# Attention values projected with tokens on partitions, page units that count as landed only with a slack, and probabilities that stay in one place

## The chip, the cores and the metric

One core of a Trainium2 chip runs the whole program. The metric is the device time of one execution in microseconds (us); for the kernel before, three runs gave 854.75, 854.88 and 855.74 us, a median of 854.88 us. The profile shown below is of one more execution of that kernel.

The core has these engines, each with its own instruction stream that runs in order: PE (matrix multiply, with a weight load stream PEld beside it), DVE (vector), ACT (scalar), POOL (general), and SP, which here only issues DMA transfers. They wait for each other through semaphores.

## The reference, cut to what matters

One inference step of a decoder layer: 256 prompt tokens and 64 sample tokens (8 requests of 8 tokens) go through one input projection of 2048 into 8272 columns; three groups of heads work on its parts; their outputs, each times a gate, go through one output projection and a layer norm. What the change touches is the value part of the first group, `av`:

```python
z = jnp.einsum('btd,dn->btn', h, w)            # tokens x 2048 by 2048 x 8272
aq, ak, av, ag, iq, ik, iw, bq, bf, bi, bg, mq, mg = jnp.split(z, cuts, axis=-1)
av = av.reshape(n_b, n_t, H_A, DH_A)           # 8 heads of 128 columns
...
p = jax.nn.softmax(s, axis=-1)
return jnp.einsum('bthk,btkhd->bthd', p, v_sel.astype(jnp.float32))
```

The prompt attends with a mask of its selected keys over its own 256 tokens. The sample tokens attend over 2048 cached keys and values each, read from pages in device memory, and over their own new keys and values. `av` itself is an output too, for prompt and sample tokens.

## The kernel before

All 320 tokens stand side by side: `xh` and `xl` hold the transposed input as a high and a low part, 16 blocks of 128 model dimensions, 320 tokens each. Every weight tile (`wr`, 512 KB, by DMA from SP) is also split, into `wh` (ACT copies, which rounds) and `wl` (DVE or POOL subtracts). A product is the sum of three PE passes: wh with xh, wh with xl, wl with xh.

Most of the input projection is done by units of 128 output columns ("T" in `pe_quantum`): the weight block is the stationary operand, the 320 tokens are streamed, and a PSUM tile `pj` (two buffers) collects 16 x 3 matmuls of 128x320. The result has columns on partitions and tokens along the row. The eight heads of `av` are eight such units; `ev_av` copies each to a tile `AV[h]` and stores it to the output `vT`. `attn_values` then turns each head by three PE transposes into tokens on partitions (`avn`; the new sample values go to `avS`), and multiplies it with the transposed probabilities.

The output projection works the other way round: the tokens are the stationary operand (three groups: tokens 0 to 127, 128 to 255, and the 64 sample tokens whose high and low part stand side by side), and 512 weight columns are streamed.

Between the quanta of the projection the PE does page units (`unit`): K units score the queries against pages of cached keys, V units multiply probabilities with pages of cached values. Each unit takes four page DMAs of 512 KB, into tiles `pg` (five buffers) or `S`. Their matmuls use 32 stationary columns at a time. A unit in one piece with the next is a pair.

No hardware queue decides the order. While the program is built, a planner (`Plan`) keeps an estimated clock for every engine; the main loop emits at each estimated moment whatever its rules call ready: background work (`bg`: the indexer, attention scores, softmax, recurrence), then page units (`units_now`), then the next projection quantum (`half_ready`), else it moves its clock on. The planner's clock is no wait on the chip. There the order is fixed and each instruction waits for its real inputs alone, so that an error of an estimate shows up as a wait of an engine behind the late instruction. `loads` sets the order of the DMAs on SP in the same way.

In the same stretch of the program DVE runs `topk_sample`: 32 rounds of a MAX8 and a MATCH_REPLACE8 over 1032 columns.

Of the kernel before, what the change touches and what calls it, by code (L numbers as in the profile page):

```python
# [47 lines left out]
IDLE = 3.0  # L48
LOOK = 3
# [96 lines left out]
class Engine:  # L146
# [41 lines left out]
    def cost(self, op, outs, ins, n):  # L188
        if self.name == "PE":
# [8 lines left out]
            if a.dtype == F32R:  # L198
                return turn + 0.0087 + n * 0.0004325
# [11 lines left out]
        f = 1.0  # L211
# [17 lines left out]
def hymba_step(ctx: ExitStack, tc: tile.TileContext, I, O):  # L229
# [199 lines left out]
    def ev_av(h):  # L429
        def f(ps):  # L430
            AV[h] = T()
            ACT.copy(AV[h], ps)
            store(O["vT"][h], AV[h])
            done.add(("av", h))
        return f
# [17 lines left out]
    def pad_queries():  # L453
        yield from wait(("mq", 0))
# [70 lines left out]
    def add_block(kind, i):  # L525
# [3 lines left out]
        elif kind == "mem":  # L529
            for k in range(16):  # L530
                wspec.append(dict(kind="mem", k=k, n=1024, nq=2, src=I["wm"][:, k, :]))
        else:
            base, ev = {"iq": (32, ev_iq), "aq": (0, ev_aq), "ak": (8, ev_ak), "av": (16, ev_av), "mq": (56, ev_mq),
# [128 lines left out]
    def page_tag(n):  # L662
# [3 lines left out]
        if (len(PG) - len(in_s) + ("q" in st) + ("more" in st) + ci_live(0) < BUFS["pg"]  # L666
                and plan.slot_free("pg", BUFS["pg"]) <= plan.now + 0.2):
            return "pg"
# [53 lines left out]
    def unit(n):  # L722
# [21 lines left out]
        elif kind == "V":  # L744
            if u == 0:
                VACC[p] = PS([128, 512], "va")
            for j in range(2):
# [31 lines left out]
    def unit_ready(n):  # L779
        kind, p, u = punits[n]  # L780
        if any((n, b) not in PG or plan.avail(PG[n, b]) > plan.now for b in range(2)):
# [5 lines left out]
        if kind == "V":  # L787
            return ("soft", p) in done and plan.avail(PTt[p]) <= plan.now and (u < 7 or "attn" in done) and (
# [8 lines left out]
    def loaded(n):  # L797
        return all((n, b) in PG and plan.avail(PG[n, b]) <= plan.now for b in range(2))
# [350 lines left out]
    def attn_scores():  # L1149
        yield from wait("pbias", "idxdone")  # L1150
        for h in range(8):
            yield from wait(("aq", h), ("ak", h))
            yield from room(2)
# [4 lines left out]
            P0, P1, s8 = T(128), T(256), T8()  # L1158
# [1113 lines left out]
```

## Time and profile before

| | us |
|---|---|
| median of three runs | 854.88 |
| the profiled execution, its own time | 854.57 |
| its span, first to last instruction | 852.8 |
| PE busy | 843.1 (99%) |
| DVE busy | 553.9 (65%) |
| ACT busy | 422.3 (50%) |
| POOL busy | 326.0 (38%) |
| DMA: hardware queue's share of 16 engines | 83.6% |

A PE row of the profile ends later than the next one starts, since matmuls are pipelined: the `pj` rows show a mean of 306 to 316 ns on the page, though they start closer together. So the cost of a matmul here is not its mean duration but the distance from one start to the next, which the chain of waits gives as a piece's time by its count. Matmuls of full fp32 operands have two rows each (three of them are `x6`); those on the split operands, and transposes, have one. PE's granted clock is 1.00 but in the last slice, when it has ended.

### The profile page before, as it was taken

What the parts mean: (1) busy time and instruction counts of PE and PEld (TensorE: products, weight loads), DVE (VectorE), ACT (ScalarE), POOL (GpSimd) and SP (SyncE); (2) the same over time, 40 slices, a digit from 0 to 9 for tenths busy, and PEclk for the clock granted to TensorE, in tenths of its full rate; (3) what the DMA queues carried; (4) which work ended last, traced back from release to release, by engine and by line L of the source; (5) the groups of instructions that cost most, each with busy time, mean ns of one, the idle gap of its engine ahead of it and who ended that gap; (6) DMA issues with size and microseconds to landing.
All of it is one profiled execution on the core that took longest, in us unless ns stands there. A gap on an engine that the chain in (4) does not pass through costs nothing.

```text
span 852.8 us, 19150 instructions
## 1 busy us (share of the span) xinstructions
PE 843.1 (99%) x6892; PEld 718.0 (84%) x6892; DVE 553.9 (65%) x1100; ACT 422.3 (50%) x908; POOL 326.0 (38%) x333
## 2 busy tenths in 40 slices
PE   9999999999999999999999999999999999999996
PEld 8999999877889898878778788787887889888885
DVE  7788897744897898654474556557545343953655
ACT  6454565553555543634544554554444353744432
POOL 0677562564634445331142214333311110714424
PEclk9999999999999999999999999999999999999998
DMA  9567456889999999999989999999999988756633
GB/s 342 172 189 228 156 172 251 279 307 411 376 389 397 335 327 359 398 360 403 389 330 409 408 353 389 401 397 377 347 409 400 364 324 291 272 171 199 195 99 123
DMA packets 83216, 266.49 MB, mean 312 GB/s; under 512 B 10481, under 2 KB 21170, under 8 KB 82482
## 3 DMA queue, kind: packets, MB, share of 16 engines
q1 hardware_dynamic: 82098, 263.18, 83.6%
q0 software_dynamic: 1024, 2.10, 0.8%
q8 instruction: 54, 0.88, 0.4%
q14 instruction: 40, 0.33, 0.1%
HBM read 256.50 MB, written 8.73 MB: 311 GB/s over the span
## 4 chain that ended last, share of the span: by engine, by line
PE 98%; DMA 1%; DVE 0%; SPq 0%; ACT 0%; DVEq 0%; issue 0%
PE pj L157 57%; PE mB L157 13%; PE va L157 10%; PE mA L157 10%; PE kv L157 8%; DMA S<-in_first 1%; DVE pg L157 0%; SPq L157 0%; ACT xh L157 0%; ACT PT L157 0%; DVE s L157 0%; DVEq L2258 0%; DVE avn L157 0%
## 5 line engine op out<-in xcount | busy, mean ns | idle before, releaser
L157 ACT CAST wh<-wr 128x512 fp32r<-128x512 f32 x334 | 205.0, 621 | 243.5 <-PE pj L157 183.9
L157 PE MATMUL pj<-xh,wh 128*128 128x320 f32 (+1 forms) x992 | 313.6, 316 | 0.0
L157 PE MATMUL pj<-xh,wl 128*128 128x320 f32 (+1 forms) x992 | 303.9, 306 | 0.0
L157 PE MATMUL pj<-xl,wh 128*128 128x320 f32 (+1 forms) x992 | 303.8, 306 | 0.0
L157 DVE TENSOR_TENSOR wl<-wr,wh 128x512 fp32r<-128x512 f32 x222 | 172.7, 785 | 181.9 <-ACT wh L157 166.5
L157 POOL TENSOR_TENSOR wl<-wr,wh 128x512 fp32r<-128x512 f32 x112 | 151.0, 1357 | 240.2 <-ACT wh L157 222.7
L157 PEld LDWEIGHTS pj<-xh,wh 128*128 128x128 f32 x992 | 186.7, 188 | 16.0 <-issue 12.5
L157 PEld LDWEIGHTS pj<-xl,wh 128*128 128x128 f32 x992 | 186.8, 188 | 1.3
L157 PEld LDWEIGHTS pj<-xh,wl 128*128 128x128 f32 x992 | 186.6, 188 | 0.0
L157 POOL TENSOR_TENSOR t<-t,t 128x256 f32<-128x256 f32 (+3 forms) x53 | 46.2, 873 | 119.5 <-ACT t L157 60.0
L157 PE MATMUL va<-pg,PT 128*32 128x512 f32 x456 | 58.4, 595 | 0.0
L157 PE MATMUL kv<-pg,qpad 128*32 128x256 f32 (+1 forms) x916 | 57.5, 380 | 0.0
L157 PEld LDWEIGHTS kv<-pg,qpad 128*32 128x32 f32 (+1 forms) x916 | 30.8, 110 | 20.4 <-issue 1.3
L157 PEld LDWEIGHTS va<-pg,PT 128*32 128x32 f32 x456 | 14.6, 109 | 30.4 <-issue 28.1
L157 DVE MAX8 PT<-PT 128x8 f32<-128x1032 f32 x32 | 39.5, 1234 | 0.5
L157 DVE MATCH_REPLACE8 PT<-PT 128x1032 f32<-128x1032 f32 x32 | 39.0, 1218 | 0.0
L157 POOL DMA_INDIRECT S<-in_ci,row x24 | 25.5, 1064 | 20.0 <-DVE row L157 10.6
L157 PE MATMUL mB<-t,wh 128*128 128x256 f32 x128 | 24.5, 289 | 0.0
L157 POOL TENSOR_TENSOR bp<-t,bp 128x128 f32<-128x128 f32 (+1 forms) x17 | 10.7, 627 | 36.0 <-ACT bp L157 36.0
L157 DVE TENSOR_TENSOR cat<-S,cat 64x512 fp32r<-64x512 f32 x24 | 19.5, 813 | 6.9 <-ACT cat L157 6.4
L157 POOL TENSOR_TENSOR t<-t,tabm 128x320 f32<-128x320 f32 x16 | 14.5, 908 | 24.4 <-DVE t L157 24.2
L157 POOL TENSOR_TENSOR xl<-cat,xh 128x256 fp32r<-128x256 f32 x12 | 12.5, 1061 | 24.8 <-ACT xh L157 24.8
(430 smaller groups left out, 1355.0 us busy)
## 6 DMA issues: line engine op xcount, KB each, us to landing
wr<-in_wt SPq DMA_DIRECT2D x124, 512.0 KB
pg<-in_ck SPq DMA_DIRECT2D x114, 512.0 KB
pg<-in_cv SPq DMA_DIRECT2D x114, 512.0 KB
wr<-in_wo SPq DMA_DIRECT2D x36, 512.0 KB
wr<-in_wm SPq DMA_DIRECT2D x16, 512.0 KB
S<-in_ck SPq DMA_DIRECT2D x14, 512.0 KB
S<-in_cv SPq DMA_DIRECT2D x14, 512.0 KB
pg<-in_cXV SPq DMA_DIRECT2D x8, 512.0 KB
```

What stands on the lines that cost most here:

```text
L157: res = f(*a, **k)
```

## The change

The eight `av` units become two chunks of 512 columns, from a weight array `wv` of another layout (the same 16 loads of 512 KB). For each of 16 blocks of model dimensions three accumulators are fed with tokens as the stationary operand: m = 0 and 1, the prompt's two halves, by three matmuls each, and m = 2, the sample tokens, by two (their high and low parts side by side in `xS`, made once by `sample_columns`). m = 0 and 1 use the two `pj` buffers, m = 2 the one `va` buffer that the V units use too. The values come out with tokens on partitions, so that `attn_values` has no transposes and no `avn`; the output is `v`, tokens by columns. V units wait until both chunks' sample values are there.

`attn_scores` writes the probabilities at once to the place in `cat` where their transposes are kept, without tiles from `t`. A page counts as landed for the planner 1.5 us later than before (`PAGE_LAG`), a weight tile's DMA is put on SP only 0.6 us after the planner thinks its buffer free (before: up to 1 us ahead), a constant `cm` is loaded early, in one DMA into a page buffer, and the planner's price of a split matmul is another formula.

```diff
 IDLE = 3.0
+PAGE_LAG = 1.5
 LOOK = 3
...
             if a.dtype == F32R:
-                return turn + 0.0087 + n * 0.0004325
+                return turn + 0.0133 + n / 2400
             if a.dtype == BF:
...
-    def ev_av(h):
-        def f(ps):
-            AV[h] = T()
-            ACT.copy(AV[h], ps)
-            store(O["vT"][h], AV[h])
-            done.add(("av", h))
+    def ev_av(n, m):
+        def f(acc):
+            ps, = acc
+            if m == 2:
+                c = slice(512 * n, 512 * n + 512)
+                ACT.copy(avS[64:128, c], ps[64:128])
+                DVE.tensor_add(avS[64:128, c], avS[64:128, c], ps[0:64])
+                store(O["v"][256:320, c], avS[64:128, c])
+                done.add(("avs", n))
+                return
+            for j in range(2):
+                AV[m, 2 * n + j] = t = T(256)
+                (DVE.tensor_copy if m else ACT.copy)(t, ps[:, 256 * j:256 * j + 256])
+                store(O["v"][128 * m:128 * m + 128, 512 * n + 256 * j:512 * n + 256 * j + 256], t)
+            if m:
+                done.update(("av", h) for h in range(4 * n, 4 * n + 4))
         return f
...
     def pad_queries():
-        yield from wait(("mq", 0))
+        yield from wait(("mq", 0), ("hgrn", 3))
         yield from room(1, "bp")
...
                 wspec.append(dict(kind="mem", k=k, n=1024, nq=2, src=I["wm"][:, k, :]))
+        elif kind == "av":
+            if i % 4 == 0:
+                for k in range(0, 16, 2):
+                    wspec.append(dict(kind="av", nch=i // 4, k=k, n=1024, nq=4,
+                                      src=I["wv"][i // 4, :, k:k + 2, :].rearrange("p a c -> p (a c)")))
         else:
-            base, ev = {"iq": (32, ev_iq), "aq": (0, ev_aq), "ak": (8, ev_ak), "av": (16, ev_av), "mq": (56, ev_mq),
+            base, ev = {"iq": (32, ev_iq), "aq": (0, ev_aq), "ak": (8, ev_ak), "mq": (56, ev_mq),
                         "bf": (44, None), "bq": (40, None), "bi": (48, None), "g": (24, None)}[kind]
...
             return None
-        if (len(PG) - len(in_s) + ("q" in st) + ("more" in st) + ci_live(0) < BUFS["pg"]
+        if (len(PG) - len(in_s) + ("cm" in st) + ("q" in st) + ("more" in st) + ci_live(0) < BUFS["pg"]
                 and plan.slot_free("pg", BUFS["pg"]) <= plan.now + 0.2):
...
                 VACC[p] = PS([128, 512], "va")
+                plan.pinned.add(VACC[p].tensor.name)
             for j in range(2):
...
         kind, p, u = punits[n]
-        if any((n, b) not in PG or plan.avail(PG[n, b]) > plan.now for b in range(2)):
+        if not loaded(n):
             return False
...
         if kind == "V":
-            return ("soft", p) in done and plan.avail(PTt[p]) <= plan.now and (u < 7 or "attn" in done) and (
+            return ("soft", p) in done and ("avs", 1) in done and plan.avail(PTt[p]) <= plan.now and (u < 7 or "attn" in done) and (
                 u or plan.slot_free("va", 1) <= plan.now)
...
     def loaded(n):
-        return all((n, b) in PG and plan.avail(PG[n, b]) <= plan.now for b in range(2))
+        return all((n, b) in PG and plan.avail(PG[n, b]) + PAGE_LAG <= plan.now for b in range(2))
...
             yield from wait(("aq", h), ("ak", h))
-            yield from room(2)
             yield need(AQ[h], AK[h], pbias)
...
             PE.matmul(ps[:, 128:384], AQ[h][:, 128:256], AK[h][:, 0:256], start=True, stop=True)
-            P0, P1, s8 = T(128), T(256), T8()
+            s8, pts = T8(), probs(h)
+            P0, P1 = pts[:, 0:128], pts[:, 128:384]
             DVE.tensor_tensor_reduce(out=P0, in0=ps[:, 0:128], in1=pbias[:, 0:128], scale=-QS, scalar=-FLOOR,
...
             PE.transpose(pt[:, 256:384], P1[:, 128:256], ident)
-            ACT.copy(probs(h), pt)
-            free(P0, P1)
+            ACT.copy(pts, pt)
             done.add(("probs", h))
+    def sample_columns():
+        yield from wait("idxdone")
+        yield from room(2, "bp")
+        xS = [new([128, 8, 128], "bp", F32R) for _ in range(2)]
+        for i in range(2):
+            for x, c in ((xh, 0), (xl, 64)):
+                (DVE.tensor_copy if c else ACT.copy)(xS[i][:, :, c:c + 64], x[:, 8 * i:8 * i + 8, 256:320])
+        st["xS"] = [x.rearrange("p k t -> p (k t)") for x in xS]
...
             yield from wait(("probs", h), ("av", h))
-            yield need(AV[h])
-            avn = new([128, 2, 128], "avn")
-            ps = PS([128, 3, 128])
-            for i in range(2):
-                PE.transpose(ps[:, i, :], AV[h][:, 128 * i:128 * i + 128], ident)
-            PE.transpose(ps[:, 2, :], AV[h][:, 192:320], ident)
-            ACT.copy(avn, ps[:, 0:2, :])
-            ACT.copy(avS[64:128, 128 * h:128 * h + 128], ps[64:128, 2, :])
-            free(AV.pop(h))
-            pts = probs(h)
-            yield need(pts, avn)
+            pts, c = probs(h), slice(128 * (h % 2), 128 * (h % 2) + 128)
+            v0, v1 = (AV[m, h // 2][:, c] for m in range(2))
+            yield need(pts, v0, v1)
             po = PS([128, 256])
-            PE.matmul(po[:, 0:128], avn[:, 0, :], pts[:, 0:128], start=True, stop=True)
-            PE.matmul(po[:, 128:256], avn[:, 0, :], pts[:, 128:256], start=True, stop=False)
-            PE.matmul(po[:, 128:256], avn[:, 1, :], pts[:, 256:384], start=False, stop=True)
+            PE.matmul(po[:, 0:128], v0, pts[:, 0:128], start=True, stop=True)
+            PE.matmul(po[:, 128:256], v0, pts[:, 128:256], start=True, stop=False)
+            PE.matmul(po[:, 128:256], v1, pts[:, 256:384], start=False, stop=True)
             cat_put(h, "p", slice(0, 256), po, ACT.copy)
+            if h % 2:
+                free(*(AV.pop((m, h // 2)) for m in range(2)))
+        yield from wait(("avs", 0), ("avs", 1))
         done.add("attn")
...
                 and plan.slot_free("pj", 2) <= plan.now
+        if s["kind"] == "av":
+            return s["k"] or q or "xS" in st and plan.avail(st["xS"][1]) <= plan.now and not pending and max(plan.slot_free("pj", 2), plan.slot_free("va", 1)) <= plan.now
         if s["kind"] == "mem":
...
                     done.add("lastT")
+        elif s["kind"] == "av":
+            n, K = s["nch"], s["k"] + q // 2
+            ms = ((0, 2), (1,)) if n == K == 0 else ((0,), (1, 2))
+            for m in ms[q % 2]:
+                if K == 0:
+                    pj["av", m] = PS([128, 512], "va" if m == 2 else "pj")
+                ps = pj["av", m]
+                t = slice(128 * m, 128 * m + 128)
+                xS = st["xS"][K // 8][:, 128 * (K % 8):128 * (K % 8) + 128]
+                xs = [(xS, hi), (xS, lo)] if m == 2 else \
+                    [(xh[:, K, t], hi), (xl[:, K, t], hi), (xh[:, K, t], lo)]
+                for x, w in xs:
+                    PE.matmul(ps, x, w, start=K == 0 and x is xs[0][0] and w is hi, stop=K == 15 and w is lo)
+                if n == 1 and K == 15 and m == 2:
+                    free(*st["xS"])
+                if K == 15:
+                    f = ev_av(n, m)
+                    if m == 2:
+                        other_bank.append(f)
+                    pending.append((f, [pj.pop(("av", m))], 0 if m == 2 else 2))
         elif s["kind"] == "mem":
...
     def masks():
-        yield from wait("idxdone")
-        yield from room(2, "bp")
-        cm = [new([128, 1024], "bp"), new([128, 1024], "bp")]
+        yield from wait(("iq", 3))
+        st["cm"] = cm = new([128, 2048], "pg")
         SP.dma_start(lbt[:, 0:8], I["lb"])
         SP.dma_start(ngt, I["ng"])
-        SP.dma_start(cm[0], I["cm"][:, 0:1024])
-        SP.dma_start(cm[1], I["cm"][:, 1024:2048])
-        yield need(*cm, lbt, ngt)
-        ACT.copy(cu8, cm[0][:, 0:304])
-        ACT.copy(emat.rearrange("p a b c d -> p (a b c d)"), cm[1])
-        free(*cm)
+        SP.dma_start(cm, I["cm"])
+        yield need(cm, lbt, ngt, ps=0)
+        yield from idle("ACT", 0.3)
+        ACT.copy(cu8, cm[:, 0:304])
+        ACT.copy(emat.rearrange("p a b c d -> p (a b c d)"), cm[:, 1024:2048])
+        del st["cm"]
         DVE.tensor_scalar(ngt, ngt, -0.5, None, op0=OP.mult)
...
                 continue
-            if nw < len(wspec) and nw < half + 5 and plan.slot_free("wr", 3) <= plan.now + 1 and nw - nprep < 3 \
+            if nw < len(wspec) and nw < half + 5 and plan.slot_free("wr", 3) <= plan.now + (-0.6) and nw - nprep < 3 \
                     and (wspec[nw]["kind"] != "mem" or has_room(3)):
...
     a["first"] = c(first.reshape(128, 8, 1312).transpose(1, 0, 2))
+    a["wv"] = c(w[:, 2048:3072].reshape(16, 128, 2, 512).transpose(2, 1, 0, 3))
     a["wm"] = c(np.concatenate([inp["w_mem_v"][0], inp["w_mem_k"][0]], 1).reshape(16, 128, 1024).transpose(1, 0, 2))
```

The order in which the instructions stand moves with it. First place: PE in the middle of the `av` projection. Before, one head's unit with a piece of attention in it (`ident,t` are the transposes of `AV[h]`, `avn` the values that they made):

```order
L157 MATMUL mA_3295<-ident,t_3217 128x128 x3
L157 MATMUL pj_3207<-xh,wh_3174 128x320
L157 MATMUL pj_3207<-xl,wh_3174 128x320
L157 MATMUL pj_3207<-xh,wl_3175 128x320
L157 MATMUL pj_3207<-xh,wh_3174 128x320
L157 MATMUL pj_3207<-xl,wh_3174 128x320
L157 MATMUL pj_3207<-xh,wl_3175 128x320
L157 MATMUL mB_3315<-cat_468_3148,avn_3294 128x128 x3
```

And now, one block of 128 model dimensions of the second chunk, for all three token groups (`bp` holds `xS`):

```order
L158 MATMUL pj_3669<-wh_3553,xh 128x512
L158 MATMUL pj_3669<-wh_3553,xl 128x512
L158 MATMUL pj_3669<-wl_3554,xh 128x512
L158 MATMUL pj_3681<-wh_3553,xh 128x512
L158 MATMUL pj_3681<-wh_3553,xl 128x512
L158 MATMUL pj_3681<-wl_3554,xh 128x512
L158 MATMUL va_3685<-wh_3553,bp_2934 128x512
L158 MATMUL va_3685<-wl_3554,bp_2934 128x512
```

In all, 384 rows of 128x320 have gone (2688 are 2304) and 256 of 128x512 have come; 24 transposes have gone (184 of 128x128 are 160).

Second place: PE between the two chunks. All three accumulators end within a few rows, and the second chunk needs them free. Between stand one K unit, the products of probabilities and values for heads 0 to 3, and another K unit; these are the rows from the end of the first unit on (`t_3576` and `t_3578` are the tiles that ACT copies from m = 0, `t_3591` and `t_3593` those that DVE copies from m = 1):

```order
L158 MATMUL kv_3597<-pg_3378,qpad_411 32x256 x2
L158 MATMUL mA_3620<-cat_459_3094,t_3576 128x128 x2
L158 MATMUL mA_3620<-cat_459_3094,t_3591 128x128
L158 MATMUL mB_3625<-cat_459_3094,t_3576 128x128 x2
L158 MATMUL mB_3625<-cat_459_3094,t_3591 128x128
L158 MATMUL mB_3630<-cat_459_3094,t_3578 128x128 x2
L158 MATMUL mB_3630<-cat_459_3094,t_3593 128x128
L158 MATMUL mA_3635<-cat_460_3095,t_3578 128x128 x2
L158 MATMUL mA_3635<-cat_460_3095,t_3593 128x128
L158 MATMUL kv_3597<-pg_3489,qpad_411 32x256 x2
```

The two K units around the products were a pair in one piece before; after the second chunk the same stands once more, for heads 4 to 7. Over the whole program, PE enters a stretch of 32-column matmuls 46 times before and 46 times now.

Third place: DVE at the same moment. The two copies of m = 1 and the sum for the sample values stand behind the scores of one head (`ISA`) and a MAX, MATCH_REPLACE round, and before the next round:

```order
L158 MAX PT_487<-PT_487 128x8
L158 MATCH_REPLACE PT_487<-PT_487 128x1032
L158 ISA cat_460_3095,s_529_3570<-mA_3567,pbias 128x128
L158 ISA s_529_3570 128x1
L158 ISA cat_460_3095,s_529_3570<-mA_3567,pbias 128x256
L158 ISA s_529_3570 128x1
L158 COPY t_3591<-pj_3117 128x256
L158 COPY t_3593<-pj_3117 128x256
L158 TENSOR_TENSOR avS<-avS,va_3112 64x512
L158 MAX PT_487<-PT_487 128x8
```

Before, no result of `av` passed DVE: ACT made all eight copies of `AV[h]`, and `avn` and `avS` too.

More of the change, by code (lines that the diff above doesn't have):

```diff
@@ L1267, in extract @@
             ACT.activation(o[i], VACC[p][:, 256 * i:256 * i + 256], AF.Copy, scale=RS[p][:, 1:2])
+        plan.pinned.discard(VACC[p].tensor.name)
         del VACC[p], PTt[p]
@@ L1373, in hgrn @@
             late_q = new([128, 2, 48], "kN")
+            done.add(("hgrn", h))
             yield from room(2, spare=spare)
@@ L1814, in ln_load @@
         if m == 0:
-            x = new([128, 2, 8, 6], "avn")
+            x = new([128, 256], "avn")[:, 0:96].rearrange("p (i a b) -> p i a b", i=2, b=6)
             st["bn"], st["bns"] = x[:, 0].rearrange("p (m a) b -> p m a b", m=2), x[:, 1]
@@ L2010, in masks @@
         done.add("masks")
-    for g in (setup(), masks(), idx_head(), idx_sample(), attn_scores(), attn_values(), *[new_keys(p) for p in range(4)],
+    for g in (setup(), masks(), idx_head(), idx_sample(), sample_columns(), attn_scores(), attn_values(), *[new_keys(p) for p in range(4)],
               *[soft(p) for p in range(4)], hgrn(), pad_queries(), *[cross_prompt(h) for h in range(4)], split()):
@@ L2021, in background @@
     def background():
-        rank = {"idx_load": 0, "idx_sample": 1, "idx_prompt": 1, "attn_scores": 2, "hgrn": 1, "xsoft": 1,
+        rank = {"idx_load": 0, "idx_sample": 1, "idx_prompt": 1, "attn_scores": 2, "sample_columns": 0, "hgrn": 1, "xsoft": 1,
                 "xextract": 1, "extract": 1, "key_scores": 0, "split": 1, "soft": 0, "attn_values": 1}
@@ L2243 @@
 _OUT = {
-    "y": (256, 2048), "ys": (128, 1024), "kT": (8, 128, 320), "vT": (8, 128, 320), "ikT": (64, 320), "sp": (4, 128, 128),
+    "y": (256, 2048), "ys": (128, 1024), "kT": (8, 128, 320), "v": (320, 1024), "ikT": (64, 320), "sp": (4, 128, 128),
     "ss": (4, 128, 8, 128), "mkT": (4, 128, 256), "mv": (256, 512),
@@ L2263 @@
     y, ys = o["y"], o["ys"].reshape(2, 64, 1024)[::-1].transpose(1, 0, 2)
-    kT, vT = o["kT"].transpose(2, 0, 1), o["vT"].transpose(2, 0, 1)
+    kT, v = o["kT"].transpose(2, 0, 1), o["v"].reshape(320, 8, 128)
     ik = o["ikT"].T
     return (c(y[None]), c(ys.reshape(8, 8, 2048)),
-            c(kT[None, None, 0:256]), c(vT[None, None, 0:256]), c(ik[None, None, 0:256]),
+            c(kT[None, None, 0:256]), c(v[None, None, 0:256]), c(ik[None, None, 0:256]),
             c(o["sp"][None, None]),
             c(o["mkT"].transpose(2, 0, 1)[None, None]), c(o["mv"].reshape(1, 1, 256, 4, 128)),
-            c(kT[256:].reshape(1, 8, 8, 8, 128)), c(vT[256:].reshape(1, 8, 8, 8, 128)),
+            c(kT[256:].reshape(1, 8, 8, 8, 128)), c(v[256:].reshape(1, 8, 8, 8, 128)),
             c(ik[256:].reshape(1, 8, 8, 64)), c(o["ss"].transpose(2, 0, 1, 3)[None]))
```

## The prediction

> **What bounds the kernel now.** I read the profile page first, then the waits of PE, then the chain of waits in order of time, then the busy time in stretches of 50 us.
>
> The page (busy time by engine; the chain that ended last, by engine and by line):
>
> ```profile
> PE 843.1 (99%) x6892; PEld 718.0 (84%) x6892; DVE 553.9 (65%) x1100; ACT 422.3 (50%) x908; POOL 326.0 (38%) x333
> ...
> PE 98%; DMA 1%; DVE 0%; SPq 0%; ACT 0%; DVEq 0%; issue 0%
> PE pj L157 57%; PE mB L157 13%; PE va L157 10%; PE mA L157 10%; PE kv L157 8%; DMA S<-in_first 1%; DVE pg L157 0%; SPq L157 0%; ACT xh L157 0%; ACT PT L157 0%; DVE s L157 0%; DVEq L2258 0%; DVE avn L157 0%
> ```
>
> All that PE waited for in this execution (total us, times, longest), and the busy time of each engine in three stretches (last: granted clock, DMA share, GB/s):
>
> ```profile
> PE kv L1947 <- DVE t L157: 1.1, 1, 1.1
> PE va L157 <- ACT PT L157: 0.6, 1, 0.6
> ...
> 250.00:300.00 50.00, 50.00 (x507) 42.46 (x506) 42.83 (x72) 27.14 (x72) 19.32 (x15) 1.00 0.96 364
> 450.00:500.00 50.00, 50.00 (x511) 41.38 (x510) 22.12 (x49) 22.38 (x54) 7.77 (x11) 1.00 1.03 410
> 800.00:852.80 52.80, 44.87 (x228) 38.22 (x227) 28.14 (x46) 17.68 (x27) 19.21 (x15) 0.95 0.37 128
> ```
>
> PE waits twice, 1.7 us together, both in the first microseconds, and is dense until the layer norm at the end; in 200 to 700 us DMA is close to full as well, but no page and no weight tile ever made PE wait. So the time is PE's work, some 844 us, plus a tail of 8 us (52.80 less 44.87 in the last row). A slack for pages has nothing to win here: there is no wait on a page to take away. What PE no longer does comes off the end, what it does more comes on, and any new wait of PE adds whole.
>
> **The prices.** From the chain in order of time (start, us, what, matmul rows). A piece by its count is the distance from one matmul to the next:
>
> ```profile
> 302.18 0.33 PE mA L157 x3
> 302.51 1.76 PE pj L157 x12
> 304.27 0.33 PE mB L157 x3
> 304.60 0.87 PE pj L157 x6
> 305.47 0.67 PE mA L157 x6
> 306.14 3.51 PE pj L157 x24
> ...
> 315.82 3.59 PE kv L157 x64
> 319.42 2.69 PE pj L157 x17
> ...
> 828.64 9.52 PE mB L157 x42
> ```
>
> 128x320: 1.76 / 12 = 0.1467 us, and 3.51 / 24 = 0.1463. 128x512 on split operands, tokens stationary as the change has it: 9.52 / 42 = 0.2267. Three transposes in the middle of `pj` (0.33) cost 0.33 with nothing on either side: the 12 `pj` rows behind them take 1.76 = 12 x 0.1467. The three probability products of a head take 0.67. A pair of K units takes 3.59, and the next piece pays for the way back: 2.69 less 17 x 0.1467 is 0.20.
>
> **The change part by part.** *The projection.* It takes away 8 heads x 16 blocks x 3 = 384 rows of 128x320: 384 x 0.1467 = 56.3 us. It adds 2 chunks x 16 x (3 + 3 + 2) = 256 rows of 128x512: 256 x 0.2267 = 58.0 us. So it costs 1.7 us: the third token group streams 512 columns for 64 tokens, and fewer, longer matmuls save only the fixed part of each, 128 times.
>
> How large is that fixed part? From the two rows, (0.2267 - 0.1467) / 192 columns = 0.417 ns a column, which leaves 13.3 ns a matmul. [...]
>
> *The transposes.* 24 of them, in 8 groups of three, leave PE: 8 x 0.33 = 2.6 us, all on the path. The probability products stay, 8 x 0.67. They now stand four heads together; since a group between `pj` rows cost nothing extra before, that saves nothing.
>
> *Stretches of page units.* Two K pairs are split around those products. The price of a split, from V units alone and in a pair:
>
> ```profile
> 204.70 1.85 PE va L157 x16
> ...
> 394.13 3.57 PE va L157 x32
> ```
>
> 2 x 1.85 - 3.57 = 0.13, plus a way back of 0.20: 0.33 each. But the order has 46 entries into such stretches before and after, since elsewhere the small products with new keys stand with units now. I take 0; the bounds are -0.3 and +0.7.
>
> *Copies off PE.* ACT made 8 copies of 128x320, 8 of `avn`, 8 of `avS`. Now ACT makes 4 of 128x256, 2 for `avS` and 2 of the 4 that build `xS`; DVE gets 4 copies of 128x256, two sums and the other 2 for `xS`. The rows:
>
> ```profile
> L157 ACT COPY t<-pj 128x320 f32<-128x320 f32 x40 | 16.7, 420 | 0.0
> ...
> L157 ACT COPY avn<-mA 128x256 f32<-128x256 f32 x7 | 2.6, 372 | 8.5 <-PE mA L157 8.5
> ...
> L157 DVE COPY t<-pj 128x256 f32<-128x256 f32 x2 | 0.7, 392 | 0.0
> ...
> L157 DVE COPY PT<-mB 128x512 f32<-128x512 f32 x5 | 3.5, 692 | 0.6 <-PE mB L157 0.6
> ```
>
> ACT is relieved by some 4 us, DVE gets about 4 x 0.39 + 4 x 0.69 = 4.3 us, under PE in the 216 to 303 us stretch. Without that cover the DVE copies would stand in PE's way, which is the next point.
>
> *The ends of the chunks: the one new wait.* Before, two `pj` buffers took turns and a head's result had the next head's 48 rows (7 us) to be copied. Now all three accumulators fall due together, twice. Between lie two rows of m = 2 (0.45 us), a K unit (1.80) and then the products, the first of which reads what DVE copies from m = 1: 2.25 us after its last matmul. Queued behind them on PE are the second K unit and the second chunk, later the recurrence's projections. DVE's rows there:
>
> ```profile
> 216.63 0.29 DVE L157 CUSTOM_DVE_ANT_0 t<-mB,pbias 128x128 f32<-128x128 f32 x1 [0.23 <-PE mB L157]
> 216.84 0.08 DVE L157 DVE_READ_ACCUMULATOR2_ANT s<- 128x1 f32 x1
> 216.84 0.42 DVE L157 CUSTOM_DVE_ANT_0 t<-mB,pbias 128x256 f32<-128x256 f32 x1
> ...
> 301.72 1.24 DVE L157 MAX8 PT<-PT 128x8 f32<-128x1032 f32 x1
> 303.00 0.09 DVE L157 MATCH_VALUE_LOAD PT<-PT 128x8 f32 x1
> 303.07 1.22 DVE L157 MATCH_REPLACE8 PT<-PT 128x1032 f32<-128x1032 f32 x1
> 304.32 1.24 DVE L157 MAX8 PT<-PT 128x8 f32<-128x1032 f32 x1
> ```
>
> A free DVE starts 0.23 us after PE and needs 2 x 0.39: 1.0 us, inside 2.25. If it has just begun a MAX, MATCH_REPLACE round (304.32 - 301.72 = 2.60), 3.6, and PE waits 1.4; with the scores' 0.65 before the copies as well, 2.0. So the wait is 0 to 2.0 at each end, 0 to 4.0 in all. I take 0.3: nearer to nothing, because in the order the round stands before the scores of a head whose matmuls end 0.7 us (three rows) ahead of m = 1's last one, and DVE was busy for 42.83 of 50 us there, not for all.
>
> *Slack, weights, masks, the place of the probabilities.* The slack and the later weight DMA put loads and units later in the order and add no instruction. SP stood for free weight buffers anyway, and ACT's casts waited for PE, rarely for a weight tile:
>
> ```profile
> SPq L157 <- DVE wl L157: 154.2, 79, 6.3
> ...
> ACT wh L157 <- PE pj L157: 183.9, 166, 4.9
> ACT wh L157 <- DMA wr<-in_wt: 11.2, 8, 2.1
> ```
>
> A tile that comes 0.6 us later falls into those 184 us. The early `cm` moves 1 MB of transfers from a stretch with a DMA share of 0.96 or more to an earlier one, which PE does not feel. Writing the probabilities in their place is the same count of the same operations. All of it: 0, with the wait of the third rival as its upper end.
>
> **Sum.** -56.3 + 58.0 - 2.6 + 0 + 0.3 = -0.6 us. The profiled execution took 854.57 us (852.8 from first to last instruction, 1.8 around it), so its like would take 853.9; the median of the runs is 0.3 above it, 854.88, and I forecast 854.2. A measurement of this kernel can tell about 0.2% from no change, 1.7 us here; the forecast is no change.
>
> **The rivals.** One more row of the chain is needed, the projection's last piece before the output projection:
>
> ```profile
> 708.64 19.36 PE pj L157 x132
> ```
>
> 1. *PE waits at the ends of the chunks* (slower). A round has just begun on DVE both times: 2 x 1.4 to 2 x 2.0 in place of 0.3, so 856.7 to 857.9, taken as 857.2. It decides from 2.4 us of wait more than I have. For it: DVE's rounds stand back to back before the second end. Against it: 2.25 us of other rows between. 0.14.
> 2. *Small delays that the chain counts as work go away* (faster). The order is new everywhere; if some 1.3 us of switching and of rows that started late are not there again, 852.9. For it: the two splits around fp32 products may cost less than 0.33. Against it: `pj` pieces between groups come out at count times price to 0.01 us. 0.17.
> 3. *Page units fall late* (slower in half of it). They end later against the projection: 60 rows (8.8 us) stand between the last unit's transposes and the output projection, 132 rows (19.36 us) before. If pages come later than that cover allows, PE waits in front of an in-order unit: from 2.4 us of wait on it is slower, 857. Against it: no page made PE wait before. 0.07.
> 4. *A matmul with tokens stationary has no fixed part to save.* Then the 128 x 13.3 ns = 1.7 us that fewer rows save are lost: 855.9, still no change. Against it: the 128x512 rows that gave 0.2267 have tokens stationary already. 0.04. [...]
>
> **How the numbers follow.** The forecast gets 0.58. Faster by over 0.2%: the second rival, 0.17. Slower: the first, and half of the third, 0.18. The rest, 0.65, is no change. The range goes from just under the second rival's 852.9 to the lower half of the first's.
>
> **What would show it.** In the profile after: `pj` and `va` pieces of 128x512 at 0.2267 a row in the chain, no transposes of `t` between them; PE busy some 1 us less; in the waits of PE, `mA` or `mB` behind a DVE copy at about 260 and 305 us if the first rival holds; `kv` or `va` behind a page DMA if the third does. I am wrong on the slow side if these waits exceed 2.4 us, on the fast side if PE's rows hold fewer than 842 us with the same counts.

## The result, and the profile after

| | before | after |
|---|---|---|
| median, the two side by side | 854.90 us | 860.79 us |
| the profiled execution, its own time | 854.57 | 861.28 |
| its span | 852.8 | 859.5 |
| first row of PE to the end of its last | 843.80 | 849.68 |
| last row of PE to the end of the span | 7.91 | 8.77 |

The ratio is 1.0067, with a 95% interval of 1.0050 to 1.0084: the change made the kernel 5.9 us slower. I had forecast 854.2 us and given "slower" 0.18; 860.8 lies above my range.

The page of the kernel after: busy time by engine, then the chain that ended last by engine and by line.

```profile
PE 846.5 (98%) x6740; PEld 707.7 (82%) x6740; DVE 555.9 (65%) x1097; ACT 419.8 (49%) x894; POOL 335.9 (39%) x344
...
PE 95%; DMA 2%; DVE 1%; POOL 1%; issue 0%; ACT 0%; SPq 0%; DVEq 0%; ACTq 0%; POOLq 0%
PE pj L158 52%; PE mB L158 12%; PE va L158 12%; PE mA L158 10%; PE kv L158 8%; DMA pg<-in_ck 1%; DMA wr<-in_wt 1%; PE kv L1993 0%; DVE t L158 0%; DVE pg L158 0%; DVE wl L158 0%; POOL S L158 0%; POOL t L158 0%; DVE bp L158 0%; SPq L158 0%
```

The chain was 98% PE before. Now DMA of weights and of pages, DVE and POOL have a share in it: PE is made to wait in the middle of the program. All its waits (total us, times, longest; "issue" is a start that came late though the engine waited for nothing that the profile shows):

```profile
PE pj L158 <- DVE t L158: 1.4, 2, 1.0
PE kv L1993 <- DVE t L158: 1.1, 1, 1.1
PE mB L158 <- DVE s L158: 0.5, 1, 0.5
PE mB L158 <- POOL t L158: 0.4, 1, 0.4
PE kv L158 <- DMA pg<-in_ck: 0.2, 1, 0.2
PE pj L158 <- DVE ngt L158: 0.2, 1, 0.2
PE mA L158 <- issue: 0.2, 1, 0.2
```

The second row was there before. The rest is new, and the five waits behind 76 us cost more than their rows say: PE is idle for 0.19 to 0.46 us there, and its next row starts 0.4 to 0.62 us late. To see what that makes in all, I added up the distances from each PE row's start to the next one's, by kind (worked out from all rows of both traces):

| rows of PE | before | after | difference |
|---|---|---|---|
| split, 128x320 | 406.92 (2688 rows) | 348.41 (2304) | -58.51 |
| split, 128x512 | 115.00 (500) | 176.05 (756) | +61.06 |
| split, 128x256 (most of them the index projection, early) | 61.95 (504) | 64.24 (504) | +2.29 |
| transposes | 18.27 (184) | 16.15 (160) | -2.12 |
| probabilities by values | 5.03 (48) | 5.75 (48) | +0.72 |
| K units and their like, 128x256 | 60.94 (1088) | 61.80 (1088) | +0.86 |
| all others together | | | +1.59 |
| PE in all | 843.80 | 849.68 | +5.89 |

With 0.86 us more behind PE's last row this is the 6.7 us by which the span grew. The split rows of the projection come out 0.9 us above the forecast, with two late starts among them (below); a row of 128x512 takes 1.36 / 6 = 0.2267 us in the chunks, as assumed (chain in order of time: start, us, rows):

```profile
227.75 1.36 PE pj L158 x6
```

**Where PE waits first.** Busy time in stretches, before:

```profile
60.00:65.00 5.00, 5.00 (x44) 5.00 (x43) 5.00 (x11) 1.82 (x3) 4.48 (x4) 1.00 0.44 144
65.00:70.00 5.00, 5.00 (x44) 5.00 (x44) 3.58 (x8) 2.29 (x4) 4.46 (x6) 1.00 0.80 252
```

and after (stretch, us, then PE, PEld, DVE, ACT, POOL, granted clock, DMA share, GB/s):

```profile
60.00:65.00 5.00, 4.66 (x37) 4.26 (x36) 2.12 (x8) 2.65 (x5) 1.41 (x2) 1.00 0.84 283
65.00:70.00 5.00, 3.78 (x28) 3.20 (x27) 4.07 (x11) 3.42 (x7) 1.87 (x3) 1.00 0.29 110
```

PE runs 65 rows in these 10 us instead of 88. What SP, ACT and DVE did there, from the order of time after (SP: issues; ACT and DVE: work, with the idle time before it and what ended it):

```profile
49.76 0.53 SPq L158 DMA_DIRECT2D wr<-in_wt  x1
...
51.30 0.42 SPq L158 DMA_DIRECT2D pg<-in_cm  x1
52.23 3.27 SPq L158 DMA_DIRECT2D S<-in_ci  x3
55.60 0.54 SPq L158 DMA_DIRECT2D wr<-in_wt  x1
```

```profile
62.33 0.62 ACT L158 CAST wh<-wr 128x512 fp32r<-128x512 f32 x1 [5.32 <-DMA wr<-in_wt]
62.86 0.44 ACT L158 CAST cu<-pg 128x304 uint8<-128x304 f32 x1
63.20 1.04 ACT L158 CAST emat<-pg 128x1024 bf16<-128x1024 f32 x1
64.15 0.62 ACT L158 CAST wh<-wr 128x512 fp32r<-128x512 f32 x1
64.79 1.28 ACT L185 ACT_TABLE_LOAD   x1
```

```profile
66.32 0.17 DVE L158 TENSOR_TENSOR lbt<-lbt 128x4 f32<-128x4 f32 x1 [0.83 <-ACT lbt L158]
...
67.02 0.51 DVE L158 STREAM_SHUFFLE t<-pj 128x320 f32<-128x320 f32 x1
```

The next weight tile is issued at 55.60, behind the 1 MB of `cm` and three transfers into `S`, and ACT stands 5.32 us for it. In the kernel before, the cast of that time waits for PE and not for its tile:

```profile
58.19 0.62 ACT L157 CAST wh<-wr 128x512 fp32r<-128x512 f32 x1 [1.14 <-PE pj L157]
```

Then, in the kernel after, `cm`'s two copies and a table load of 1.28 us stand among the casts, and the copy that frees a `pj` waits on DVE behind the small constants, which wait for that table. In the early stage PE loses 2.70 us on the 128x256 rows (by the same distances, up to 100 us; those behind 500 us gain 0.41, which makes the table's 2.29). At 75.7 us a row of small products starts another 0.55 us late, behind POOL; that wait is in this kernel alone (it is gone with `cm` late, but also with `cm` early and the weights ahead), so its cause stays open.

**And at the start of the first chunk.** DVE after (start, us):

```profile
220.87 1.22 DVE L158 MAX8 PT<-PT 128x8 f32<-128x1032 f32 x1
...
222.20 1.22 DVE L158 MATCH_REPLACE8 PT<-PT 128x1032 f32<-128x1032 f32 x1
223.46 0.29 DVE L158 CUSTOM_DVE_ANT_0 cat<-mB,pbias 128x128 f32<-128x128 f32 x1
...
224.03 0.52 DVE L158 STREAM_SHUFFLE t<-pj 128x320 f32<-128x320 f32 x1
224.44 0.47 DVE L158 TENSOR_TENSOR t<-pj,tabm 128x320 f32<-128x320 f32 x1
```

The chunk needs both `pj` buffers. The second still holds the last head of `ak`, whose copy is behind a round of 2.6 us and a head's scores. PE's next row comes 0.55 us late.

### The profile page after: what moved, and what is told of

The parts are those of the page before. It is cut to its first block, busy times and chain, and to the rows that moved or that the text cites. A ratio compares the mean times of both kernels' runs of the same rounds, so it can differ in the third digit from the quotient of the medians.

```text
span 859.5 us, 18856 instructions
## 1 busy us (share of the span) xinstructions
PE 846.5 (98%) x6740; PEld 707.7 (82%) x6740; DVE 555.9 (65%) x1097; ACT 419.8 (49%) x894; POOL 335.9 (39%) x344
## 4 chain that ended last, share of the span: by engine, by line
PE 95%; DMA 2%; DVE 1%; POOL 1%; issue 0%; ACT 0%; SPq 0%; DVEq 0%; ACTq 0%; POOLq 0%
PE pj L158 52%; PE mB L158 12%; PE va L158 12%; PE mA L158 10%; PE kv L158 8%; DMA pg<-in_ck 1%; DMA wr<-in_wt 1%; PE kv L1993 0%; DVE t L158 0%; DVE pg L158 0%; DVE wl L158 0%; POOL S L158 0%; POOL t L158 0%; DVE bp L158 0%; SPq L158 0%
## 5 line engine op out<-in xcount | busy, mean ns | idle before, releaser
L158 PE MATMUL pj<-xh,wh 128*128 128x320 f32 (+1 forms) x864 | 272.1, 315 | 1.2 <-DVE t L158 1.0
L158 POOL TENSOR_TENSOR wl<-wr,wh 128x512 fp32r<-128x512 f32 x118 | 158.0, 1347 | 283.1 <-ACT wh L158 216.4
L158 PE MATMUL pj<-xh,wl 128*128 128x320 f32 (+1 forms) x864 | 264.8, 306 | 0.4 <-DVE ngt L158 0.2
L158 PE MATMUL pj<-xl,wh 128*128 128x320 f32 (+1 forms) x864 | 264.4, 306 | 0.0
L158 PEld LDWEIGHTS pj<-xh,wh 128*128 128x128 f32 x864 | 162.6, 188 | 19.5 <-issue 14.8
L158 PEld LDWEIGHTS pj<-xl,wh 128*128 128x128 f32 x864 | 162.8, 188 | 1.1
L158 PEld LDWEIGHTS pj<-xh,wl 128*128 128x128 f32 x864 | 162.6, 188 | 1.0 <-DVE wl L158 1.0
L158 PE MATMUL pj<-wh,xh 128*128 128x512 f32 x64 | 27.0, 422 | 0.4 <-DVE t L158 0.4
L158 PE MATMUL pj<-wl,xh 128*128 128x512 f32 x64 | 25.0, 391 | 0.0
L158 PE MATMUL pj<-wh,xl 128*128 128x512 f32 x64 | 25.0, 391 | 0.0
```

What stands on the lines that cost most here:

```text
L158: res = f(*a, **k)
```

## The experiments

Medians are in us, beside the median of the kernel before that was timed together with each, with the 95% interval of the ratio. Idle times, ends and waits are those of one profiled execution of each kernel; the executions of one kernel can differ by more than that (before_w_late: 856.6 to 860.8 us in ten). "Idle" is the time after 20 us in which no row of PE runs (before: 0.03; after: 3.20); it leaves out the late starts behind a wait.

| run | median | before | ratio, 95% | idle of PE | end of PE's last row |
|---|---|---|---|---|---|
| after | 860.79 | 854.90 | 1.0050-1.0084 | 3.20 | 850.7 |
| after_w_ahead | 860.72 | 855.26 | 1.0043-1.0077 | 2.87 | 850.3 |
| after_cm_late | 858.81 | 855.26 | 1.0026-1.0049 | 1.64 | 848.6 |
| before_w_late | 858.11 | 855.26 | 1.0024-1.0046 | 3.10 | 849.1 |
| before_cm_early | 859.70 | 855.26 | 1.0036-1.0069 | 2.67 | 849.7 |
| projection_alone | 864.40 | 854.89 | 1.0091-1.0125 | 5.23 | 854.7 |
| after_cm_used_later | 859.65 | 854.89 | 1.0034-1.0074 | 2.53 | 849.0 |
| after_chain_without_cm | 858.96 | 854.89 | 1.0031-1.0063 | 2.82 | 848.6 |
| before_w_late_slack | 864.16 | 854.89 | 1.0095-1.0129 | 5.26 | 852.2 |
| before_new_price | 859.50 | 854.84 | 1.0030-1.0064 | 2.30 | 851.0 |
| before_slack | 863.08 | 854.84 | 1.0071-1.0121 | 5.20 | 854.0 |
| projection_with_slack | 863.68 | 854.84 | 1.0085-1.0119 | 5.42 | 853.2 |
| after_cm_late_no_slack | 864.51 | 854.84 | 1.0093-1.0127 | 5.41 | 855.1 |
| cm_late_two_pj_free | 860.77 | 855.00 | 1.0049-1.0082 | 3.36 | 850.2 |
| cm_late_w_03 | 858.53 | 855.00 | 1.0028-1.0062 | 0.79 | 847.7 |
| cm_late_slack_2 | 859.66 | 855.00 | 1.0036-1.0070 | 2.35 | 849.5 |
| cm_late_slack_3 | 859.64 | 855.00 | 1.0041-1.0074 | 2.98 | 849.5 |

### One part undone, one part alone: the weights' lead and `cm`

```diff
# after_w_ahead (on the kernel after; before_w_late is the reverse on the kernel before)
-plan.slot_free("wr", 3) <= plan.now + (-0.6)
+plan.slot_free("wr", 3) <= plan.now + 1
# after_cm_late (on the kernel after; before_cm_early is the reverse)
-        yield from wait(("iq", 3))
-        st["cm"] = cm = new([128, 2048], "pg")
+        yield from wait("idxdone")
+        yield from room(2, "bp")
+        cm = [new([128, 1024], "bp"), new([128, 1024], "bp")]
...
```

> The changed kernel with one part undone: a weight tile's DMA is again put on SP up to 1 us ahead of the moment at which the planner thinks its buffer free; the early load of `cm`, the page slack and the new projection stay. Theory A (the later weight DMA starves the casts and so PE at 55 to 76 us; the trace after shows about 3 us of PE gaps there): 857.5 us, no `wr<-in_wt` piece in the chain before 80 us, PE busy 5.00 in each 5 us from 50 to 80 us. Theory B (the 1 MB of `cm` ahead of the weights in SP's queue does it): 860.8 us, the piece stays. Theory C (the loss lies in the projection's chunks): 860.8 us.

> The changed kernel with one part undone: `cm` is loaded as before, in two halves into `bp` after the index work; the later weight DMA stays. Theory A: 860 to 861 us, PE's gaps at 55 to 76 us stay. Theory B: 857.5 us, the gaps are gone. If it takes both together (a weight tile that is put on the queue late, behind 1 MB of other data): 857.5 us here and with the weights ahead as well. Theory C: 860.8 us with the gaps gone.

> The kernel before with one part of the change alone: a weight tile's DMA is put on SP 0.6 us after the planner thinks its buffer free. Theory A: 857.9 us (854.9 + 3), PE waits for late weights at 55 to 76 us. Theory B and C: 854.9 us. My prediction's step on this part (0): 854.9 us.

> The kernel before with one part of the change alone: `cm` is loaded early in one DMA of 1 MB into a page buffer. Theory A: 854.9 us. Theory B: 857.9 us with PE gaps at 55 to 76 us. Both together needed: 854.9 us here and 854.9 us with the weights late alone. My prediction's step (0): 854.9 us.

The stretches 60 to 70 us, with `cm` late:

```profile
60.00:65.00 5.00, 5.00 (x43) 5.00 (x42) 5.00 (x12) 1.86 (x3) 4.41 (x3) 1.00 0.39 130
65.00:70.00 5.00, 5.00 (x44) 5.00 (x44) 3.66 (x8) 2.28 (x4) 4.41 (x6) 1.00 0.79 258
```

and in the kernel before with `cm` early:

```profile
60.00:65.00 5.00, 4.78 (x38) 4.45 (x37) 2.85 (x11) 2.46 (x5) 2.19 (x2) 1.00 0.78 271
65.00:70.00 5.00, 3.80 (x28) 3.22 (x27) 4.07 (x11) 3.54 (x6) 1.69 (x2) 1.00 0.36 124
```

The gaps are there exactly where `cm` is early, whatever the weights' lead: theory B holds for this place and theory A falls. Undoing it gave 2.0 us back (860.79 to 858.81), somewhat less than the 2.7 us that the stretch had lost. But before_w_late was slower as well, by 2.9 us, and not at 62 us: one page came late, at 230 us.

```profile
PE kv L157 <- DMA pg<-in_ck: 3.1, 1, 3.1
```

Neither theory has that. And before_cm_early lost 4.4 us, more than the early stretch holds: it has a second wait, 1.0 us at 652 us behind a DVE operation.

### What of `cm`: its transfer, or the work with it

```diff
# after_cm_used_later (on the kernel after; the tile is held meanwhile)
         SP.dma_start(cm, I["cm"])
+        plan.pinned.add(cm.tensor.name)
+        t = plan.now
+        while plan.now < t + 24.0:
+            yield
         yield need(cm, lbt, ngt, ps=0)
...
# after_chain_without_cm (on the kernel after; what does not use cm stays where it is)
         yield from wait(("iq", 3))
-        st["cm"] = cm = new([128, 2048], "pg")
         SP.dma_start(lbt[:, 0:8], I["lb"])
         SP.dma_start(ngt, I["ng"])
-        SP.dma_start(cm, I["cm"])
...
+        yield from wait("idxdone")
+        yield from room(2, "bp")
+        cm = [new([128, 1024], "bp"), new([128, 1024], "bp")]
...
```

> The changed kernel, `cm` loaded just as early, but what uses it and the small constants (two ACT copies, a table load, the short DVE chain of the lower bounds) is emitted 24 us later. Theory D (the 1 MB transfer makes a weight tile land late): PE's gaps at 62 to 69 us stay, PE busy about 8.4 of 10 us in 60 to 70 us, 860.8 us. Theory E (the copies and the table load stand ahead of the weight casts on ACT, and the DVE chain behind them ahead of the copy that frees a `pj`): the gaps at 62 to 69 us are gone, 10.0 of 10 us, and the time is about 858.5 us, if the chain does no harm 24 us later.

> The changed kernel, `cm` and its two copies late as before, but the small constants with their table load and DVE chain early. Theory D: no gaps at 62 to 69 us, 858.5 us. Theory E in its narrow form (the table load and the chain alone are enough): the longest gap, 1.2 us at 66.7, stays; 860 us. If both the late tile and the chain are needed, the gaps are gone here and in the run with `cm` used later.

With `cm` used later, PE in the same stretches:

```profile
60.00:65.00 5.00, 4.65 (x36) 4.24 (x35) 3.38 (x9) 2.21 (x4) 2.02 (x2) 1.00 0.85 289
65.00:70.00 5.00, 5.00 (x44) 5.00 (x43) 5.00 (x10) 2.40 (x5) 4.30 (x4) 1.00 0.67 223
```

With the chain alone, both stretches are full (5.00 and 5.00). So both theories hold in part. The transfer alone costs the 0.35 us of idle before 65 us; the long gap behind 65 us needs the late weight tile and the chain together, since either alone leaves none there. after_cm_used_later is still at 859.65 (two executions); its trace has a page wait of 1.2 us at 530 us, which the kernel after had as 0.2.

### The projection by itself, the slack by itself

```diff
# projection_alone (on the kernel after: weights ahead, cm late as above, and)
-PAGE_LAG = 1.5
+PAGE_LAG = 0
...
-                return turn + 0.0133 + n / 2400
+                return turn + 0.0087 + n * 0.0004325
# before_w_late_slack, before_slack (on the kernels before_w_late and before)
+PAGE_LAG = 1.5
...
-        if any((n, b) not in PG or plan.avail(PG[n, b]) > plan.now for b in range(2)):
+        if not loaded(n):
...
-        return all((n, b) in PG and plan.avail(PG[n, b]) <= plan.now for b in range(2))
+        return all((n, b) in PG and plan.avail(PG[n, b]) + PAGE_LAG <= plan.now for b in range(2))
```

> The changed kernel with every other part undone (weights ahead, `cm` late, no slack for pages, the old price of a split matmul): what is left is the values' projection with tokens on partitions and the probabilities in their place. My prediction's sum for this part is -0.6 us: 854.7 us beside a before of 855.3. Theory from the traces (with `cm` late the changed kernel still took 3.5 us more than before, spread over the chunks at 200 to 325 us and over single waits of 0.3 to 0.7 us of PE elsewhere): 857.5 to 858.5 us.

> The kernel before with the later weight DMA and with the slack of 1.5 us for pages, no other part. With the weights late alone PE waited 3.1 us for one page of a K unit at 230 us. If the slack is what keeps a unit from coming ahead of its page: no such wait, 855.3 us. If it only moves units without regard to that: the wait stays, 858 us.

Both missed by far, on the slow side: 864.4 and 864.2 us. What PE waited for with the projection alone:

```profile
PE mB L158 <- ACT t L158: 2.5, 1, 2.5
PE kv L158 <- DMA pg<-in_ck: 2.3, 2, 1.3
```

The projection without the change's other parts is the slower kernel. (Here, in before_slack and in after_cm_late_no_slack one wait is followed by 3.4 us in which PE's granted clock is 0.50, by estimate some 1.7 us of loss that is neither wait nor work; the last section shows it.) And on the kernel before with late weights, the slack left a page wait at 230 us (1.7 us of 3.1) and added one of 2.8 us at 532 us. So I formed a new theory, R: the order before is one that holds no wait of PE after the first microseconds; any other plan of nearly the same work brings single waits of 0.3 to 3 us behind a page, a copy or a cast, wherever its estimates miss. Its rival, theory S, is that each part of the change has its own cost and a new order none. The sharpest test is a change that touches no instruction:

```diff
# before_new_price (on the kernel before)
-                return turn + 0.0087 + n * 0.0004325
+                return turn + 0.0133 + n / 2400
```

> The kernel before with only the planner's price of a split matmul replaced by the change's formula (0.1466 in place of 0.1471 us for 128x320, 0.2266 in place of 0.2301 for 128x512): no instruction more or less, another order from about two thirds of the PE's rows on. Theory R (the order before holds no wait of PE by fortune of its tuning, and a new plan brings single waits of 0.3 to 3 us behind a page, a copy or a cast): 856 to 860 us, with one to three such waits. Theory S (each part of the change has its own cost, a new order none): 855.0 us.

> The kernel before with only the slack of 1.5 us for pages. My prediction's step: 854.9 us, nothing to win, since no page made PE wait. Theory R: 856 to 860 us with single waits of PE in places that differ from those of the other kernels, also ones that are no page's. Theory S: 855 us, or if a slack by itself delays the units, waits at pages that are the same as with the weights late.

> The projection alone (864.4 us, page waits of 1.5 us at 220 and 1.1 us at 531, a wait of 2.7 us behind a copy at 604) with the slack of 1.5 us for pages added. If the slack keeps units behind their pages, the two page waits go: 861.7 us, and 859.0 us if the new order also loses the wait at 604. Theory R: 857 to 864 us, waits in other places.

> The changed kernel with `cm` late and without the slack (the weights still late). With the slack it took 858.8 us and no page made PE wait. If the slack is what kept page waits away: one or two page waits of 1 to 3 us at about 220 to 230 and 531 us come, 861 to 863 us. If not: 858.8 us.

before_new_price: the same work, 4.7 us slower. The largest of its waits that the kernel before does not have:

```profile
PE pj L157 <- ACT t L157: 0.8, 1, 0.8
PE va L157 <- DMA pg<-in_cv: 0.6, 2, 0.4
PE mA L157 <- ACT t L157: 0.5, 1, 0.5
```

They sit together: PE is busy for 8.06 of the 10 us from 630 to 640 us, and for 10.00 in the kernel before. A V unit's page comes late while DMA is full (a share of 1.02 in these 10 us), and a short chain between PE and ACT behind it finds no cover. By the usual distances of such rows (means over all traces of this case), some 4 us are lost between 628 and 637 us alone: an estimate. The order has a second price: PE enters a stretch of 32-column matmuls 49 times here, 46 in the kernel before, about 1 us at the prediction's 0.33 each. Theory R holds, with switches beside the waits; S falls. before_slack says the same, with page waits that the kernel before does not have:

```profile
PE kv L158 <- DMA S<-in_ck: 2.7, 1, 2.7
PE kv L158 <- DMA pg<-in_ck: 1.8, 1, 1.8
```

Yet within the changed kernel the slack mostly does what its name says. With `cm` late and no slack there are three page waits of 4.6 us together, with it none; and it takes both page waits from projection_alone (where the new order has other waits, of 2.0 and 1.1 us behind ACT and DVE). Why the same slack brings page waits to the kernel before was not settled.

### Other orders of the changed kernel

```diff
# on the kernel with cm late: cm_late_two_pj_free, cm_late_w_03, cm_late_slack_2 and _3
-max(plan.slot_free("pj", 2), plan.slot_free("va", 1)) <= plan.now
+max(plan.slot_free("pj", 2), plan.slot_free("va", 1)) <= plan.now and plan.n_free("pj", 2) == 2
-plan.now + (-0.6)
+plan.now + (-0.3)
-PAGE_LAG = 1.5
+PAGE_LAG = 2.0        # 3.0
```

> The changed kernel with `cm` late, and a chunk of the values' projection starts only when the planner thinks both `pj` buffers free (it asked for one). In the trace with `cm` late PE stands 0.39 us at the chunk's start for a DVE copy that is behind a MAX8 and MATCH_REPLACE8 round. If that is the cause, this wait is gone. If the time is the sum of the projection's own cost and of waits: 858.3 us if the rest of the order holds, anything from 857 to 864 us if the new order brings waits of its own.

> The changed kernel with `cm` late and the weights' DMA 0.3 instead of 0.6 us late: only 34 rows of PE's order move, all after 570 us; SP's order changes in a few places. Order theory: the waits before 570 us stay as they are (0.39 at 221 us), those at 572, 594 and 639 us (0.36, 0.55, 0.34) may change; 857.5 to 860 us. Projection theory: 858.8 us.

> The changed kernel with `cm` late and a slack of 2.0 instead of 1.5 us. Order theory: other single waits of PE after about 400 us, 857 to 864 us, and the time above 856.5 is the sum of these waits within 1 us. Projection theory: 858.8 us whatever the waits.

> The changed kernel with `cm` late and a slack of 3.0 us. Pages are then counted later still: if a slack as such removes page waits, none are left; the stretches of V and K units move from about 200 us on. Order theory: 857 to 864 us by the single waits. Projection theory: 858.8 us.

With the two-buffer condition PE does not wait for `pj` at the chunk's start any more, so that cause is shown; the new order brings others, one at a page in spite of the slack:

```profile
PE kv L158 <- DMA pg<-in_ck: 1.5, 1, 1.5
...
PE mB L158 <- ACT t L158: 0.8, 1, 0.8
```

cm_late_w_03, with 34 rows of PE moved, is the fastest of the changed kernels. All that is left in it:

```profile
PE kv L1993 <- DVE t L158: 1.1, 1, 1.1
PE va L158 <- ACT PT L158: 0.5, 1, 0.5
PE pj L158 <- DVE t L158: 0.4, 1, 0.4
PE va L158 <- ACT t L158: 0.3, 1, 0.3
```

Its first two rows are those of the kernel before. Between the five kernels of this family with a slack, PE's end goes with its idle time (0.79, 1.64, 2.35, 2.98, 3.36 us idle; 847.7, 848.6, 849.5, 849.5, 850.2 us), as the order theory says; after_chain_without_cm, with `cm` late too, does not fit (2.82 us idle, 848.6). But with 0.79 us idle cm_late_w_03 is still 3.5 us slower, where I had expected the time above 856.5 to be the sum of such waits. By the table of distances, cm_late_w_03 against before: split rows -58.81 + 61.46 = +2.65, transposes -1.77, probabilities by values +0.35, all others +1.57, PE together +2.80; and the tail is 0.36 longer. Of this, 0.79 is idle time and up to 1 us can be the order's switches (PE enters 32-column stretches 49 times here as well); the rest would be the projection's own, which no run separates. None of the versions beats the kernel before.

## Why the prediction was wrong

**The bound: right.** PE bounds the kernel; everything that it waited (idle for 3.20 us, 0.03 in the kernel before, by the table of the runs) came on whole, and late starts on top.

**The projection's price: right.** 0.2267 and 0.1467 us were measured again. I put +1.7 us on the end; the rows' distances grew by 61.06 - 58.51 = 2.55 us. Two late starts are counted in them: 0.55 us at the first chunk's start, and 0.62 at 714 us, where the row ahead of two late transposes is one of 128x320. Without them the rows cost 1.4 us. The fixed part of 13.3 ns a matmul, an estimate from the two distances, stands with them.

**The transposes: nearly right.** -2.6 forecast, -2.12 measured, and the probability products became dearer by 0.72 (a head's products that follow 32-column matmuls directly take 0.86 us, the others 0.67), which I had put at 0. Together -1.4 in place of -2.6. The table counts by row, so a part of what a switch costs stands with the split row behind it; the sum of the three lines is firmer than each.

**The ends of the chunks: no wait there; the rival's mechanism, at another place.** No row of PE waits behind the copies of `m = 1`. But a MAX8 and MATCH_REPLACE8 round stood ahead of the copy of the last `ak` head, at the first chunk's start, and cost 0.55 us. I had looked at what the chunk leaves behind, not at what it finds: the diff asks for one free `pj` where the chunk takes two.

**"Slack, weights, masks, the place of the probabilities: 0": this step failed.** It held three claims. "The early `cm` moves 1 MB of transfers from a stretch with a DMA share of 0.96 or more to an earlier one, which PE does not feel": PE felt it with 2.0 us (what undoing it gave back) to 2.7 us (the rows of that stretch), by a weight tile that came late and by `cm`'s copies and the table load among the casts. I had priced the transfer's bandwidth and forgotten that a moved step takes its ACT and DVE work along. "A tile that comes 0.6 us later falls into those 184 us": in the changed kernel so, 860.72 with the weights ahead against 860.79; but alone on the kernel before the later weights cost 2.9 us, through a page. And "the slack and the later weight DMA put loads and units later in the order and add no instruction": true, and no reason for 0. before_new_price adds no instruction either and costs 4.7 us. I took the order's freedom from waits for a property of the kernel; it was one of that one order, and every other plan that was timed lost it.

**The rivals.** The first (PE waits at the ends of the chunks, 857.2) had the mechanism in another place and a fifth of the size. The third (units late, 857) shows in little: PE's rows around 531.9 us come 0.4 us late for a page, in mid-program, not at the end that it named. The second, that small delays vanish, came out the other way round; the fourth did not occur. I had no rival "the new order has waits of its own", though the forecast had said "the order is new everywhere".

The 6.7 us between the two profiled executions, then: 2.7 early by `cm`; 0.55 at 75.7 us, of open cause; 0.55 at the first chunk's start; 0.62 at 714 us; nothing by the projection and its products apart from these two, where I had put -0.9 (2.55 - 0.55 - 0.62 - 2.12 + 0.72 = -0.02); 0.86 behind PE's last row. The remaining 1.5 are late starts at 532 and 648 us (0.4 each) and small differences of both signs that were not followed. The tail's cause stays open: the chain behind PE is the same row by row, and the difference lies after DVE's last row and the last issue. Open too is what a search for good constants would reach for the changed kernel; seven orders of it with `cm` late and a slack gave 858.5 to 863.7.

## What to carry to other kernels

Where a planner's estimates fix the order, a change of the order has a price of its own, which no count of instructions shows: here 3 to 9 us in each of the five other plans of the kernel before that were timed, even the one with the same instructions. So compare a changed kernel with several plans of both, and read its single waits of PE, before the change itself is judged. A load that is moved earlier brings its consumers along: look at which queue of casts and copies they enter. And a rule that starts a piece of work must ask for all the buffers that the piece takes.

## What the runs showed of the hardware

**After three waits of 2.1 to 2.7 us PE's granted clock was 0.50 for 3.41 us.** before_slack, where a page comes 2.7 us late at 533 us (the granted clock stands ahead of the DMA share):

```profile
534.00:536.00 2.00, 0.26 (x7) 0.23 (x11) 0.40 (x2) 0.00 (x0) 0.00 (x0) 1.00 1.04 404
536.00:538.00 2.00, 2.00 (x28) 1.13 (x20) 0.00 (x0) 0.00 (x0) 0.00 (x0) 0.66 1.03 410
538.00:540.00 2.00, 2.00 (x8) 1.25 (x5) 0.00 (x0) 0.00 (x0) 0.00 (x0) 0.50 1.02 408
540.00:542.00 2.00, 2.00 (x16) 1.87 (x15) 0.61 (x1) 1.25 (x3) 0.26 (x1) 0.99 1.04 406
```

For 3.41 us, from 536.64 us on, the granted clock is 0.50: half of that, by estimate 1.7 us, is lost on top of the wait. It happened after idle times of 2.09 us (after_cm_late_no_slack), 2.54 (projection_alone) and 2.67 (before_slack), and not after others of 2.00 and 2.01 (cm_late_slack_3 and projection_with_slack, one each), 2.24 (after_cm_late_no_slack), 2.79 (before_w_late_slack) and 3.06 (before_w_late); none of the waits under 1.8 us showed it. The slow stretch was 3.41 us long each of the three times. The executions of before_slack differ in their clock too: 861.44 us at a mean granted clock of 0.998, 865.83 at 0.993. What decides whether such a wait is followed by a slow stretch, no run here shows.

**A DVE operation beside one of POOL took four times as long, 1.41 us for 0.35.** The wait at 714 us in the kernel after, two like rows of DVE:

```profile
713.18 1.41 DVE L158 TENSOR_SCALAR t<-t,s 128x256 f32<-128x256 f32 x1
...
714.69 0.35 DVE L158 TENSOR_SCALAR t<-t,s 128x256 f32<-128x256 f32 x1
```

and POOL's row there:

```profile
713.14 1.29 POOL L158 TENSOR_TENSOR wl<-wr,wh 128x512 fp32r<-128x512 f32 x1 [7.51 <-ACT wh L158]
```

DVE's row ends 0.15 us after POOL's (by the rows before rounding), and the transposes that wait for DVE's result come 0.62 us late. It is no single case: in the eighteen traces 22 such DVE rows run beside such a POOL row and outlast it, 20 of them by 0.15 us and two by 0.26, while those that meet no POOL row mostly take 0.35 us. The kernel before has one too, of 1.03 us at 655.8, for which PE does not wait. Why such a row ends only after POOL's, no run here shows.
